# Second norm and first query moved into the output projection, queries of both block groups in one chain, and the gathered blocks' scores searched from SBUF

## The chip, the cores and the metric

The kernel runs on one core of a Trainium2 chip, as one program. The metric is the device time of one execution in microseconds (us). The engines are named as in the profile: PE is the matrix engine (PEld its weight loads), DVE the vector engine, ACT the scalar engine, POOL the GpSimd engine, and SP the engine that issues most of the DMAs. Each engine takes its instructions in the order of the program; semaphores join the engines.

## What is computed

One layer on 1024 tokens of width 1024, in float32. Two mixers (a gated linear recurrence and a chunked state-space scan) each give 512 columns; these are normed, multiplied by an output matrix and added to the input. Then follows a retrieval layer ("PEER"), which is what the change is about:

```python
h = h + y @ w_out                        # y: the two normed groups side by side
x = rms_norm(h, norm2_g)
q = (x @ wq).reshape(T, 8, 256)          # 8 heads, two halves of 128 each
s1 = einsum('thd,kd->thk', q[..., :128], k1)   # 128 scores for each half
s2 = einsum('thd,kd->thk', q[..., 128:], k2)
v1, i1 = top_k(s1, 16); v2, i2 = top_k(s2, 16)
sc, cidx = top_k(v1[..., :, None] + v2[..., None, :], 16)   # best 16 of the 256 pairs
e = i1[cidx // 16] * 128 + i2[cidx % 16]                    # an expert of 16384
g = softmax(sc)
out = sum over h, k of g * gelu(u_tab[e] . x) * v_tab[e]
result = rms_norm(h + out, normf_g)
```

## The kernel before, in words

**Tiling.** The tokens are 8 blocks of 128. Blocks 0 to 4 (`dblocks`, ND = 5) are dense blocks: all 16384 experts are computed for them by matmuls, with the chosen weights spread out as a matrix G. Blocks 5 to 7 (`gblocks`, NG = 3) are gathered blocks: for each token the 128 chosen rows of the two expert tables are fetched by POOL's indirect DMAs (2 x 128 transfers of 512 KB for a block, line 1146) and multiplied on DVE, with eight row buffers (`rows`). Every float32 product runs as three float32r matmuls, of a high and a low part; ACT makes the high part by a copy, DVE the low part by a subtraction (names ending in h and l).

**Order.** Each piece of work is a Python generator, and `Merge` (lines 62 to 118) interleaves several of them as the program is written: it keeps an estimated clock for each engine, and always takes the generator whose own clock plus a bias is lowest. A generator that yields a name waits until that flag is set. What stands in each engine's queue is fixed by this.

**Output projection** (`front`, lines 757 to 841). `wo_half` loads and splits the eight 128x512 pieces of one half of w_out, with ten buffers for the split pieces (tags woh and wol) and two for the raw ones (wor). `norm` gives the group's row factors rg (a matmul with ones into gs, then a root and small DVE steps). `w_out` goes through the blocks from 7 down to 0, two column halves each: 12 matmuls into wop, then DVE adds wop times rg into h. After the second half, ACT sums the squares of h[b] into ss (jk). The two PSUM buffers of wop are the tag pj.

**Second norm and queries** (`peer`, lines 856 to 972). All pools of `front` are closed first. `norm2` scales and transposes first blocks 5 to 7, then 0 to 4: rsqrt_cols on ss, xn on DVE (line 905), for the gathered blocks two stores (X_d, H_d), then eight PE transposes into x2t and the split into xGh and xGl, or xDh and xDl. `query` goes over 8 heads and two halves: weights (wqr by SP, split into wqh and wql one query ahead, two buffers), 24 matmuls into qp (twice for the dense blocks, 320 columns each), a copy to qt, and for each block two matmuls with the keys kT into sp, a copy to sc, and a store of sc to S_d in DRAM. It runs first for the gathered blocks (pool pqa), and after all pools of this stage have been closed a second time for the dense blocks (pool pqb).

**Choice** (`topk`, lines 983 to 1066). The 1 MB of a block's scores comes back from S_d (s). For each head and half, DVE finds the 16 largest of 128 (two rounds of MAX8 and FIND_INDEX8 with a MATCH_REPLACE8 between). Then it adds the candidate pairs (cd), searches them in the same way (scv, ci), and turns positions into indices with one-hot products (oh, if). For a gathered block the result is idx (flag g0 to g2), which the gathers wait for; for a dense block `build_g` transposes it, and makes 32 groups of one-hot matrices (ohA, ohB) for G. In the stage of the dense queries three threads run together: `dense_query`, `topks` (gathered blocks 5, 6, 7), and `gathers`. After it come `build`, the first layer of the dense experts for 97 of 128 tiles (`ahead`: ur, uh, ul, ap, stored as A_d), and at last the dense loop over 32 chunks (`dense`: vp), which takes in the remaining gathered rows.

Of the kernel before, what the change touches and what calls it, by code (L numbers as in the profile page):

```python
# [21 lines left out]
L = 8  # L22
# [127 lines left out]
def front(tc, a, cst, nd, mg):  # L150
# [608 lines left out]
    pools.close("fl", "fw", "fin", "fxa")  # L759
    pa_ = pools.open("fa")  # L760
    ah = pa_.tile([P, 4, T], F32R, name="ah")
    al = pa_.tile([P, 4, T], F32R, name="al")
    po = pools.open("fo")
# [4 lines left out]
    def wo_half(half):  # L768

        for k in range(4):  # L770
            for n in range(2):
# [39 lines left out]
    def w_out(half):  # L811
# [3 lines left out]
        for b in reversed(range(L)):  # L815
            bs = slice(b * P, b * P + P)
            for n in range(2):
                ns = slice(512 * n, 512 * n + 512)
                pp = pj("wop")
                for k in range(4):  # L820
                    wh, wl = wo[half][k, n]
                    PE.matmul(pp, dh[:, k, bs], wl, start=(k == 0), stop=False)
                    PE.matmul(pp, dl[:, k, bs], wh, start=False, stop=False)
                    PE.matmul(pp, dh[:, k, bs], wh, start=False, stop=(k == 3))
                yield
                V.scalar_tensor_tensor(h[b][:, ns], pp, rg[half][:, b:b + 1], h[b][:, ns], ALU.mult, ALU.add)
                yield
            if half:
                jk = po.tile([P, D], F32, name="jk", tag="sq2")
                S.activation(jk, h[b], AF.Square, accum_out=ss[:, b:b + 1])  # L830
                yield

    def group_a():
        yield from wo_half(0)
        yield from w_out(0)
        yield from wo_half(1)
# [19 lines left out]
def peer(tc, a, cst, pools, h, ss, mg):  # L856
# [9 lines left out]
    dr = pools.open("dram", space=DRAM)  # L866
    S_d = dr.tile([8, P, 8, 256], F32, name="S_d")
    X_d = dr.tile([NG, P, D], F32, name="X_d")
    H_d = dr.tile([NG, P, D], F32, name="H_d")
# [19 lines left out]
    pxg = pools.open("pxg")  # L889
    xGh = pxg.tile([P, 8, TG], F32R, name="xGh")  # L890
    xGl = pxg.tile([P, 8, TG], F32R, name="xGl")
    pn = pools.open("pn", "right", bufs=2)
    g2 = pn.tile([P, D], F32, name="g2", bufs=1)
    S.dma_start(g2, a["g2"].partition_broadcast(P))
    vv = pn.tile([P, 8], F32, name="vv", bufs=1)
    r2 = pn.tile([P, 8], F32, name="r2", bufs=1)
# [734 lines left out]
```

## Time and profile before

| | us |
|---|---|
| median of 3 runs (lowest, highest) | 2759.59 (2755.72, 2765.24) |
| the profiled execution, and its span | 2759.9, 2758.1 |
| busy in the span: PE, DVE | 2538.0 (92%), 2364.1 (86%) |
| busy in the span: ACT, POOL | 1329.9 (48%), 1164.7 (42%) |
| mean granted clock of PE | 0.964 of full speed |

How to read it: the profile is one execution, and times in it count from the start of its span. Nearly every instruction is issued through one helper and so carries the line L146; instructions are told apart by their tiles, written out<-in. "Idle before" is time in which the engine had nothing to do before an instruction, and the name behind it is what it waited for. The chain of waits is followed back from the last instruction of the program, at each step to what released it.

### The profile page before, as it was taken

What the parts mean: (1) busy time and instruction counts of PE and PEld (TensorE: products, weight loads), DVE (VectorE), ACT (ScalarE), POOL (GpSimd) and SP (SyncE); (2) the same over time, 40 slices, a digit from 0 to 9 for tenths busy, and PEclk for the clock granted to TensorE, in tenths of its full rate; (3) what the DMA queues carried; (4) which work ended last, traced back from release to release, by engine and by line L of the source; (5) the groups of instructions that cost most, each with busy time, mean ns of one, the idle gap of its engine ahead of it and who ended that gap; (6) DMA issues with size and microseconds to landing.
All of it is one profiled execution on the core that took longest, in us unless ns stands there. A gap on an engine that the chain in (4) does not pass through costs nothing.

```text
span 2758.1 us, 40787 instructions
## 1 busy us (share of the span) xinstructions
PE 2538.0 (92%) x14623; PEld 2289.4 (83%) x14623; DVE 2364.1 (86%) x4540; ACT 1329.9 (48%) x2407; POOL 1164.7 (42%) x777
## 2 busy tenths in 40 slices
PE   5979879887899999989989889999999999999997
PEld 5767769787898999988989878888788888888885
DVE  6888634699998999989989869999788889999996
ACT  5456424222294693955846734444443334434432
POOL 0000000044373575856836634455445555445550
PEclk9999889999999999999999999999999999999998
DMA  5111233375799898997998999999889999999993
GB/s 167 29 38 33 105 136 125 127 256 180 267 366 371 287 401 323 353 392 266 397 334 293 400 343 328 328 328 327 321 316 327 330 328 333 334 327 327 327 343 134
DMA packets 302139, 761.83 MB, mean 276 GB/s; under 512 B 28784, under 2 KB 126384, under 8 KB 296816
## 3 DMA queue, kind: packets, MB, share of 16 engines
q0 software_dynamic: 110592, 402.70, 40.8%
q1 hardware_dynamic: 184464, 345.19, 35.3%
q10 hardware_dynamic: 6880, 11.33, 1.2%
q8 instruction: 115, 1.88, 0.3%
q14 instruction: 88, 0.72, 0.1%
HBM read 668.81 MB, written 89.13 MB: 275 GB/s over the span
## 4 chain that ended last, share of the span: by engine, by line
PE 57%; DVE 25%; DMA 9%; issue 5%; ACT 3%; POOL 1%; SPq 0%; ACTq 0%; DVEq 0%; POOLq 0%
PE vp L146 24%; PE ap L146 15%; PE total L146 6%; DVE row L146 5%; PE wop L146 3%; PE qp L146 3%; DMA A_d<-aa 3%; PE gp L146 2%; DVE ix L146 2%; DVE oh L146 2%; DVE ul L146 2%; DMA ur<-in_uT_dram 2%; DVE v L146 2%; PE pj L146 1%; DVE hb L146 1%
## 5 line engine op out<-in xcount | busy, mean ns | idle before, releaser
L1146 POOL DMA_INDIRECT row<-in_peer_u_dram,idx x384 | 581.6, 1515 | 1014.4 <-DVE ix L146 521.6
L1146 POOL DMA_INDIRECT row<-in_peer_v_dram,idx x384 | 580.3, 1511 | 477.9 <-DVE hb L146 364.2
L146 PE MATMUL ap<-xDl,uh 128*128 128x320 f32 x2048 | 654.8, 320 | 16.3 <-ACT aa L146 16.1
L146 PE MATMUL ap<-xDh,ul 128*128 128x320 f32 x2048 | 650.5, 318 | 20.4 <-DVE ul L146 20.3
L146 PE MATMUL ap<-xDh,uh 128*128 128x320 f32 x2048 | 646.9, 316 | 0.0
L146 DVE SCALAR_TENSOR_TENSOR hb<-row,act,hb 128x1024 f32<-128x1024 f32 x384 | 492.2, 1282 | 6.6 <-DMA hb<-H_d 2.2
L146 DVE CUSTOM_DVE_ANT_0 row<-row,xg 128x1024 f32<-128x1024 f32 x384 | 458.5, 1216 | 7.7 <-DMA xg<-X_d 4.9
L146 PEld LDWEIGHTS ap<-xDh,ul 128*128 128x128 f32 x2048 | 392.2, 192 | 25.5 <-DVE ul L146 24.1
L146 PE MATMUL vp<-vl,hh 128*128 128x512 f32 x1024 | 400.3, 391 | 12.6 <-DVE h L146 10.4
L146 PEld LDWEIGHTS ap<-xDl,uh 128*128 128x128 f32 x2048 | 392.4, 192 | 19.7 <-ACT aa L146 17.7
L146 PE MATMUL vp<-vh,hl 128*128 128x512 f32 x1024 | 400.1, 391 | 0.0
L146 PE MATMUL vp<-vh,hh 128*128 128x512 f32 x1024 | 400.1, 391 | 0.0
L146 PEld LDWEIGHTS ap<-xDh,uh 128*128 128x128 f32 x2048 | 391.6, 191 | 0.0
L146 ACT ACTIVATE gq<-gt 128x640 f32<-128x640 f32 x128 | 175.1, 1368 | 337.7 <-DVE hr L146 335.8
L146 PE MATMUL gp<-ohB,ohA 128*128 128x128 f32 x1280 | 211.0, 284 | 43.0 <-ACT gs L146 24.8
L146 DVE TENSOR_TENSOR ul<-ur,uh 128x1024 fp32r<-128x1024 f32 x128 | 156.1, 1219 | 108.5 <-ACT uh L146 108.4
L146 PEld LDWEIGHTS vp<-vl,hh 128*128 128x128 f32 x1024 | 193.0, 188 | 54.1 <-DVE h L146 11.7
L146 PEld LDWEIGHTS gp<-ohB,ohA 128*128 128x128 f32 x1280 | 186.8, 194 | 52.8 <-ACT gs L146 27.0
L146 PEld LDWEIGHTS vp<-vh,hh 128*128 128x128 f32 x1024 | 193.0, 188 | 40.3
L146 PEld LDWEIGHTS vp<-vh,hl 128*128 128x128 f32 x1024 | 193.1, 189 | 39.4
L146 ACT ACTIVATE aa<-ap 128x320 f32<-128x320 f32 x194 | 85.0, 439 | 267.8 <-PE ap L146 250.1
L146 ACT ACTIVATE ohB<-ohB,kt 128x128 f32<-128x128 f32 x480 | 204.4, 503 | 0.0
(424 smaller groups left out, 4512.8 us busy)
## 6 DMA issues: line engine op xcount, KB each, us to landing
ur<-in_uT_dram SPq DMA_DIRECT2D x128, 512.0 KB, 6.6
vr<-in_peer_v_dram SPq DMA_DIRECT2D x128, 512.0 KB, 6.5
gt<-G_d SPq DMA_DIRECT2D x32, 1280.0 KB, 9.5
G_d<-gs SPq DMA_DIRECT2D x19, 2048.0 KB, 25.4
A_d<-aa SPq DMA_DIRECT2D x96, 320.0 KB, 7.4
hr<-A_d SPq DMA_DIRECT2D x96, 320.0 KB, 5.7
wqr<-in_wq_dram SPq DMA_DIRECT2D x32, 512.0 KB, 4.2
S_d<-sc SPq DMA_DIRECT2D x64, 128.0 KB, 3.7
```

Source lines behind the costliest of these rows:

```text
L146: return fn(*args, **kw)
L1146: G.indirect_dma_start(out=r, out_offset=None, in_=a["peer_v" if at >= P else "peer_u"], in_offset=bass.IndirectOffsetOnAxis(ap=idx[n][:, ...
```

## The change

1. **Projection.** The pool of the output weights is opened before that of ah and al, so that the latter can be closed after the first half. `wo_half` goes over columns first; the weights of the second half may be loaded once the first columns of the first half (flag cols0), or all of it (half0), have been used, and `w_out(0)` goes through all blocks for the first columns and then for the second.
2. **Norm and first query in `front`.** A new class `Norm2` holds the second norm. For blocks 7, 6 and 5 it runs beside the second half's lower blocks, as soon as flags h7 to h5 are set. `query0` loads the first of the 32 query weights into buffers of the output weights, and computes the first query of the gathered blocks (q0) behind the projection.
3. **One query chain.** `query` runs through the gathered and then the dense blocks, with weights loaded one query ahead across the seam. The norm of the dense blocks is a thread beside it.
4. **Search from SBUF.** The gathered blocks' scores are not stored to S_d; sc stays in one of six buffers, and the thread `found_g` searches head by head, into tiles vg and ixg kept for `topk`, which for these blocks starts with the candidates once flag "found" is set.
5. **Pools and biases.** rows, gp and pu lie on the other side of the memory; `topks` and `gathers` have the biases 1.0 and 2.0, and the dense query is no thread of this run.

The core of the diff (the changes of names and pools that only follow from it are left out):

```diff
     def wo_half(half):
-        for k in range(4):
-            for n in range(2):
+        for n in range(2):
+            for k in range(4):
+                if half:
+                    yield "half0" if (n, k) >= (1, 2) else "cols0"
...
-        for b in reversed(range(L)):
+        todo = [(b, n) for b in reversed(range(L)) for n in range(2)]
+        if half == 0:
+            todo.sort(key=lambda x: x[1])
+        for b, n in todo:
...
+            if half == 0 and (b, n) == (0, 0):
+                mg.flag("cols0")
+            if half and n:
                 jk = po.tile([P, D], F32, name="jk", tag="sq2")
                 S.activation(jk, h[b], AF.Square, accum_out=ss[:, b:b + 1])
+                mg.flag(f"h{b}")
                 yield
+        mg.flag(f"half{half}")
...
-    mg.run([(0.5, norm(0, yA, ah, al)), (1.0, group_a())])
-    pools.close("fo", "fa", "fgw", "fg", "fvt", "fkeep", "fps")
-    return pools, h, ss
+    mg.run([(0.5, norm(0, yA, ah, al)), (1.0, group_a()), (1.0, wo_half(1))], until="half0")
+    pools.close("fa")
+    nx = Norm2(tc, a, cst, pools, h, ss, mg)
+
+    def query0():
+        hi, lo = [], []
+        for i in range(2):
+            r = po.tile([P, 512], F32, name="wor", tag="wor", bufs=2)
+            nc.sync.dma_start(r.rearrange("p (k n) -> p k n", n=P), a["wq"][0][:, 4 * i:4 * i + 4])
+            yield "half0"
+            wh = po.tile([P, 512], F32R, name="woh", tag="woh", bufs=10)
+            wl = po.tile([P, 512], F32R, name="wol", tag="wol", bufs=10)
+            S.activation(wh, r, AF.Copy)
+            V.tensor_tensor(wl, r, wh.bitcast(F32), ALU.subtract)
...
+        yield "xg"
+        yield "half1"
+        p_ = pt("qp")[:, :TG]
+        for k in range(8):
+            PE.matmul(p_, hi[k], nx.xGl[:, k], start=(k == 0), stop=False)
+            PE.matmul(p_, lo[k], nx.xGh[:, k], start=False, stop=False)
+            PE.matmul(p_, hi[k], nx.xGh[:, k], start=False, stop=(k == 7))
+        yield
+        S.activation(nx.q0, p_, AF.Copy)
+        mg.flag("query0")
+
+    def norm2_g():
+        for b in range(ND, L):
+            yield f"h{b}"
+        yield from nx.run(list(range(ND, L)), nx.xGh, nx.xGl, pt)
+        mg.flag("xg")
...
+    mg.run([(0.5, norm2_g()), (1.5, query0_late())], until="query0")
+    mg.run([], until="half1")
...
+    def run(self, blocks, dh, dl, pt):
+        mg, nc, h = self.mg, self.tc.nc, self.h
+        sl = slice(blocks[0], blocks[-1] + 1)
+        rsqrt_cols(mg, self.vv[:, sl], self.r2[:, sl], self.ss[:, sl], 1.0 / D)
+        yield
+        for n, b in enumerate(blocks):
+            xn = self.pn.tile([P, D], F32, name="xn", tag="xn")
+            mg.V.scalar_tensor_tensor(xn, h[b], self.r2[:, b:b + 1], self.g2, ALU.mult, ALU.mult)
+            yield
+            if b >= ND:
+                nc.sync.dma_start(self.X_d[b - ND], xn)
+                nc.sync.dma_start(self.H_d[b - ND], h[b])
...
+        nxt = weights(1)
+        yield
+        for part, (blocks, dh, dl) in enumerate(((gblocks, nx.xGh, nx.xGl), (dblocks, xDh, xDl))):
...
+            if part:
+                mg.flag("qg")
+                yield "xd"
...
+                    sc = pq.tile([P, 256], F32, tag="sc", name="sc", bufs=6)
+                    S.activation(sc, p_[:, :256], AF.Copy)
+                    if part:
+                        nc.sync.dma_start(S_d[b, :, h_], sc)
+                    else:
+                        scs[h_, n] = sc
...
+    def found_g():
+        for h in range(8):
+            for n in range(NG):
+                yield lambda: (h, n) in scs
+                sc = scs.pop((h, n))
                 for f in range(2):
+                    top16(sc[:, f * P:(f + 1) * P], found[n][0][:, f, h], found[n][1][:, f, h])
                 yield
+        mg.flag("found")
+
+    mg.run([(0.0, norm2_d()), (0.5, query()), (1.0, found_g())], until="xd")
+    mg.run([], until="qg")
+    pools.close("pn", "pxg", "hg")
...
     def topk(b):
+        if b >= ND:
+            yield "found"
+            v, ix = found[b - ND]
...
-    mg.run([(0.0, dense_query()), (0.5, topks()), gr], until="q")
-    pools.close("pqb")
+    mg.run([(1.0, topks()), gr], until="q")
+    mg.run([], until="chosen")
+    pools.close("pkg", "pq")
```

What this does to the engines' queues is seen at two places. On PE, at the end of the output projection, the queue before has the 24 transposes of the gathered blocks' norm (x2t) behind the last projection matmul (wop, second half: gh, gl), and then the first query (qp) with its weights wqh and wql:

```order
L146 MATMUL wop<-wol,gh 128x512
L146 MATMUL wop<-woh,gl 128x512
L146 MATMUL wop<-woh,gh 128x512
L146 MATMUL x2t<-ident,xn 128x128 x24
L146 MATMUL qp<-xGl,wqh 128x384
L146 MATMUL qp<-xGh,wql 128x384
L146 MATMUL qp<-xGh,wqh 128x384
```

In the changed kernel the first 16 transposes stand in the middle of the second half:

```order
L146 MATMUL wop<-wol,gh 128x512
L146 MATMUL wop<-woh,gl 128x512
L146 MATMUL x2t<-ident,xn 128x128 x8
L146 MATMUL wop<-woh,gh 128x512
L146 MATMUL x2t<-ident,xn 128x128 x8
L146 MATMUL wop<-wol,gh 128x512
L146 MATMUL wop<-woh,gl 128x512
```

The last eight follow 13 matmuls behind these, and the projection's last matmul is followed directly by the first query, whose weights lie in buffers named woh and wol:

```order
L146 MATMUL wop<-woh,gl 128x512
L146 MATMUL wop<-woh,gh 128x512
L146 MATMUL qp<-xGl,woh 128x384
L146 MATMUL qp<-xGh,wol 128x384
L146 MATMUL qp<-xGh,woh 128x384
```

So the norm's transposes moved from behind the projection into it, and the first query moved up to its end. On DVE, the queue before searches the gathered scores only after all gathered queries, from the tile s that came back from DRAM, between weight splits (wql) of the dense queries, and goes on to the candidates (cd):

```order
L146 TENSOR_TENSOR wql<-wqr,wqh 128x1024
L146 MAX v<-s 128x8 x2
L146 MAX_INDEX ix<-v,s 128x8 x2
L146 MAX v<-s 128x8 x2
L146 MAX_INDEX ix<-v,s 128x8 x2
L146 MATCH_REPLACE s<-v,s 128x128 x2
L146 MAX v<-s 128x8 x2
L146 MAX_INDEX ix<-v,s 128x8 x2
```

In the changed kernel, in the middle of the gathered queries, one head of all three blocks is searched from sc (tiles vg_3311, vg_3313 and vg_3315) between two pairs of weight splits:

```order
L146 TENSOR_TENSOR wql<-wqr,wqh 128x1024 x2
L146 MAX vg_3311<-sc 128x8 x2
L146 MAX_INDEX ixg_3312<-vg_3311,sc 128x8 x2
L146 MATCH_REPLACE sc<-vg_3311,sc 128x128 x2
L146 MAX vg_3311<-sc 128x8 x2
L146 MAX_INDEX ixg_3312<-vg_3311,sc 128x8 x2
...
L146 MATCH_REPLACE sc<-vg_3315,sc 128x128 x2
L146 MAX vg_3315<-sc 128x8 x2
L146 MAX_INDEX ixg_3316<-vg_3315,sc 128x8 x2
L146 TENSOR_TENSOR wql<-wqr,wqh 128x1024 x2
```

So the search of the gathered scores moved ahead by the whole gathered query stage, with two weight splits before each head of it. Counted over DVE's whole queue, the third idx stands behind 22 gathered rows instead of 33, the first one-hot of the build behind 61 instead of 50, and the dense loop's first addition behind 398 instead of 393 (the first low part of v there behind 393 instead of 388).

More of the change, by code (lines that the diff above doesn't have):

```diff
@@ L886, in split_to, with norm2_d, query @@
         V.tensor_tensor(lo, src, hi.bitcast(F32), ALU.subtract)
[L889 to L896, printed above, removed]
[L898 to L927 removed]
+    pq = pools.open("pq", bufs=2)
+    def norm2_d():
+        yield from nx.run(dblocks, xDh, xDl, pt)
+        mg.flag("xd")
+    def query():
         kT = pq.tile([P, 2, P], F32, name="kT", bufs=1)
@@ new lines, in query, with top16 @@
+        mg.flag("q")
+    pkg = pools.open("pkg")
+    found = [(pkg.tile([P, 2, 8, 16], F32, name=f"vg{n}"), pkg.tile([P, 2, 8, 16], U32, name=f"ixg{n}"))
+             for n in range(NG)]
+    scs = {}
+    def top16(x, vals, at):
+        for r in range(2):
+            vs = vals[:, 8 * r:8 * r + 8]
+            V.max(vs, x)
+            V.max_index(at[:, 8 * r:8 * r + 8], vs, x)
+            if r == 0:
+                V.match_replace(x, vs, x, -3.0e38)
+    def found_g():
[3 more added lines that the diff above has]
+                sc = scs.pop((h, n))
@@ L962, in query @@
                 for f in range(2):
-                    PE.matmul(p_[:, f * P:(f + 1) * P], qs[f][:, n * P:(n + 1) * P], kT[:, f], start=True, stop=True)
+                    top16(sc[:, f * P:(f + 1) * P], found[n][0][:, f, h], found[n][1][:, f, h])
                 yield
-                sc = pq.tile([P, 256], F32, tag="sc", name="sc", bufs=4)
-                S.activation(sc, p_[:, :256], AF.Copy)
-                nc.sync.dma_start(S_d[b, :, h_], sc)
-                yield
-    pqa = pools.open("pqa", "right", bufs=2)
@@ L971, in peer @@
-    mg.run([(0.0, norm2()), (0.5, query(pqa, gblocks, xGh, xGl))])
-    pools.close("pqa", "pn", "hg", "pxg")
-    rows = pools.open("rows", bufs=ROWS)
-    gp = pools.open("gp", bufs=2)
-    pu = pools.open("pu", bufs=2)
+        mg.flag("found")
+    mg.run([(0.0, norm2_d()), (0.5, query()), (1.0, found_g())], until="xd")
+    mg.run([], until="qg")
+    pools.close("pn", "pxg", "hg")
+    rows = pools.open("rows", "right", bufs=ROWS)
+    gp = pools.open("gp", "right", bufs=2)
+    pu = pools.open("pu", "right", bufs=2)
@@ L1009, in topk @@
         for h in range(8):
[L1010 to L1016 removed]
+            top16(cd[:, h], sc[:, h], ci[:, h])
             yield
@@ L1562, in body @@
     cst = dict(ident=ident, iota=iota)
[L1563 to L1564 removed]
+    fpools, h, nx = front(tc, a, cst, ND, mg)
+    peer(tc, a, cst, fpools, h, nx, mg)
     pools.close("cst")
```

186 lines of the change are left out of this document (89 added, 97 removed).

## The prediction

> **What bounds the kernel now.** I read the busy time of the engines by stretches first, then the chain of waits through the stretches that the change touches, then the instructions there one by one. In the stretches the columns are start and end, length, busy time (and instructions) of PE, PEld, DVE, ACT and POOL, granted clock, DMA share and GB/s.
>
> ```profile
> 398.00:511.26 113.26, 93.86 (x544) 89.27 (x544) 41.50 (x55) 41.91 (x76) 0.00 (x0) 0.89 0.43 139
> 511.26:561.10 49.84, 44.23 (x285) 42.84 (x286) 49.55 (x251) 15.12 (x29) 0.00 (x0) 0.90 0.39 129
> 561.10:688.60 127.50, 104.80 (x693) 101.16 (x692) 126.62 (x510) 30.55 (x67) 56.06 (x37) 0.93 0.68 226
> 688.60:750.00 61.40, 52.59 (x327) 50.83 (x328) 61.40 (x250) 15.68 (x25) 19.22 (x18) 0.94 0.77 260
> ...
> 1200.00:1300.00 100.00, 95.52 (x644) 93.80 (x644) 97.25 (x287) 45.67 (x94) 57.32 (x29) 0.98 0.87 304
> 1300.00:1400.00 100.00, 86.67 (x600) 84.16 (x599) 84.98 (x152) 83.20 (x218) 71.35 (x49) 0.93 1.04 391
> ...
> 2000.00:2400.00 400.00, 396.42 (x1922) 341.00 (x1923) 357.40 (x471) 161.99 (x177) 207.12 (x142) 0.99 0.91 326
> ```
>
> Four regimes stand here. From 398 to 511 (norm and queries of the gathered blocks) DVE works 41.5 of 113.3 us, and PE has most of the work. From 511 to 750 DVE is never idle (176.2 of 177.3 us, then 61.4 of 61.4): it searches scores, and PE waits for it. From there to about 1640 DVE and PE are each near 90 to 97%, and in some stretches the DMA engines are full (1.04). After 1640 PE sets the time (396.4 of 400). So an idle DVE lies directly before a full one.
>
> The chain (start, length, what) shows what the idle stretch consists of:
>
> ```profile
> 349.03 4.03 DMA ur<-in_uT_dram
> 356.11 41.45 PE wop L146 x174
> 399.61 5.41 DMA g<-in_g_dram
> ...
> 406.36 5.20 DMA X_d<-xn
> ...
> 416.11 11.32 PE qp L146 x48
> ...
> 485.16 7.28 PE qp L146 x42
> 495.07 7.30 PE qp L146 x42
> 505.16 1.86 DMA S_d<-sc
> 507.21 6.53 DMA wqr<-in_wq_dram
> ...
> 562.32 4.24 DMA row<-in_peer_u_dram,idx
> ...
> 1640.94 12.28 PE vp L146 x54
> ```
>
> Output projection until 397.6, then a DMA and a norm with PE idle until the queries at 416.1; a gathered head takes 9.91 us (485.16 to 495.07); then a store and a weight load at the seam before the dense queries; the first gather only at 562.3, and the dense loop (vp) from 1640.9. Who waited there:
>
> ```profile
> PE qp L146 <- DVE wql L146: 22.5, 7, 9.6
> PE qp L146 <- ACT wqh L146: 10.2, 1, 10.2
> ...
> DVE v L146 <- DMA s<-S_d: 16.1, 1, 16.1
> ```
>
> **The change, part by part.** The sum is made against the profiled execution: span 2758.1 us, its own time 2759.9, which is 0.3 above the median of the runs (2759.59). I count how much earlier fixed places in the program are reached.
>
> The prices come from these rows: instructions in order of time (start, length, and idle before), then groups (shortest, median and longest ns), and one DMA issue with its us to landing.
>
> ```profile
> 397.16 0.39 PE L146 MATMUL wop<-woh,gh 128*128 128x512 f32 x1
> 421.08 0.52 PE L146 MATMUL qp<-xGl,wqh 128*128 128x384 f32 x1
> 421.40 0.52 PE L146 MATMUL qp<-xGh,wql 128*128 128x384 f32 x1
> 426.93 0.33 PE L146 MATMUL qp<-xGh,wql 128*128 128x384 f32 x1
> 427.10 0.34 PE L146 MATMUL qp<-xGh,wqh 128*128 128x384 f32 x1
> 427.27 1.03 PE L146 MATMUL x2t<-ident,xn 128*128 128x128 f32 x8
> 428.07 0.42 PE L146 MATMUL qp<-xGl,wqh 128*128 128x384 f32 x1
> ```
>
> ```profile
> 511.26 0.49 DVE L146 MAX8 v<-s 128x8 f32<-128x128 f32 x2 [16.09 <-DMA s<-S_d]
> ...
> 513.61 0.47 DVE L146 MAX8 v<-s 128x8 f32<-128x128 f32 x2
> ...
> 755.36 0.70 DVE L146 TENSOR_TENSOR ohA<-iota,kt 128x512 f32<-128x512 f32 x1
> ```
>
> ```profile
> L146 DVE SCALAR_TENSOR_TENSOR xn<-h,r,g x8: 1274/1283/1286, 405.0 to 440.4; 128x1024 f32<-128x1024 f32 x8
> L146 ACT ACTIVATE wqh<-wqr x32: 1047/1052/1071, 404.8 to 660.1; 128x1024 fp32r<-128x1024 f32 x32
> L146 DVE TENSOR_TENSOR wql<-wqr,wqh x32: 1193/1222/1251, 406.2 to 669.5; 128x1024 fp32r<-128x1024 f32 x32
> L146 DVE CAST idx<-if x3: 205/209/261, 561.1 to 688.6; 128x128 int32<-128x128 f32 x3
> L146 DVE CUSTOM_DVE_ANT_0 row<-row,xg x384: 1192/1217/1296, 566.6 to 2354.9; 128x1024 f32<-128x1024 f32 x192
> ```
>
> ```profile
> wqr<-in_wq_dram SPq DMA_DIRECT2D x32, 512.0 KB, 4.2
> ```
>
> *Weights of the second half.* The columns-first order frees four weight buffers early, and the ur loads leave this place, so the wait that ended at 356.1 can shrink. But the two splits of the first query's weights now stand ahead of the last step of the half's own rg on DVE, and behind that step wait both PSUM buffers of wop. Bounds: the seven microseconds from 349.0 to 356.1 gone, or 3 more. I take −2, nearer to nothing, because the same rg chain still ends it.
>
> *Norm inside the second half.* Its 24 transposes cost PE 3 × 0.80 (427.27 to 428.07) = 2.4 us among the wop matmuls. Added are waits: for xn of block 5 behind a square, a root and five small DVE steps, with 2 units of wop ahead on PE; and for the third xn, whose buffer is free only when the X_d store (5.20) landed. DVE stands still meanwhile, with the h update behind it that frees a wop buffer. I take +5 in all (bounds +2.4 and +11). The projection so ends at 397.6 − 2 + 5 = 400.6.
>
> *First query in front, next weights.* Its 24 matmuls follow at once. The next weights wait for the projection's end as the first did before: 0.5 to issue, 4.2 to land, 1.05 and 1.22 to split: 407.6. PE is idle about 3 us of it. The spacing of matmuls was 0.32 us after the 9 us gap (421.08 to 421.40) and 0.17 later (426.93 to 427.10), so the second query takes 7.7 us slow or 4.2 fast. I take 7.7: it ends at 415.3, where before both had ended at 427.3, 12 us earlier. The Trainium skill (TensorE: Matmul & The Clock Gate, What's actually happening) says that about 3.4 us of idleness halves the clock and as much work restores it. By that page the shorter gap may leave the clock up, and the place would be reached 3.5 us sooner; the trace shows only the long gap.
>
> *The seam.* Store, pool change and weight load between 502 and 514.9 go, as queries run on. PE then starts the dense queries at 514.9 − 12 − 11.5 = 491. It worked 44.2 + 104.8 = 149 us from 511.3 to 688.6; so the place of 688.6 comes at 640 at the earliest on PE, 49 sooner (53 with the fast clock).
>
> *Searches moved.* One head of one block takes 2.35 us (511.26 to 513.61); 24 of them, 56.4 us, move under the gathered queries. A head there costs DVE 3 × 2.35 + 2 × 1.22 = 9.5 us against PE's 9.91, so the cover just holds, and the norm of the dense blocks comes on top. DVE's work from 398 to 688.6 is 41.50 + 49.55 + 126.62 = 217.7. Out of it go 3 × 1.28 of xn, about 3.7 of the six xGl (taken as half a wql each) and 1.2 of the first split, all now ahead of the projection's end: 209. With 11 us idle (4 until the first weights land, 7 waiting for scores; bounds 4 and 30) DVE is at the place of 688.6 by 400.6 + 209 + 11 = 621, 68 sooner. If the cover failed, DVE would keep part of its old idle time. The stores and loads of S_d that go (24 and 3 on SP) lay in a stretch with DMA share 0.4.
>
> *After the third idx.* In the order, the first one-hot of the build (755.36) has 61 rows of the gather ahead of it instead of 50, so DVE is there 68 − 11 × 1.217 = 55 sooner. PE had 8.8 us idle in 688.6 to 750 and can be there 49 to 58 sooner. At the head of the dense loop 393 rows are done instead of 388: DVE could be 62 sooner, PE not more than 58. I take 55. The dense loop then has 5 rows less; PE sets it, so that is worth 0.
>
> Sum: 2759.9 − 55 = **2705**.
>
> **The rivals.** *Transfers set it.* The row gathers cannot begin before the first idx; searches end near 501 (400.6 + 41.5 − 8.7 + 56.4 + 11), and what followed them for block 5 took from 530 (511.3 + 8 × 2.35) to 561, so the first gather comes at 532, only 30 sooner. If bytes bound everything from there to 1640, the gain is 30: 2730. For it: 1.04 in 1300 to 1400. Against: 0.87 in the stretch before, 0.68 in 561 to 688. The Trainium skill (DMA: Bandwidth & Descriptors, Issuing engines are not separate DMA queues) says that all queues end on the same 16 engines, so gathers that start beside the query weights get no bandwidth of their own; by it this rival is what a full stretch would do.
>
> *Searches stop the queries: slower.* DVE takes its instructions in order. If a search stood ahead of the weight split that PE needs next, each gathered head would be in series: 9.91 + 7.05 + 1.22 = 18.2 instead of 9.91, 8 × 8.3 = 66 us more, 2705 + 66 = 2771. It decides from 9.91 + 55/8 = 16.8 us a head. Against it: two splits stand ahead of each head's searches in the order, and PE has two queries (8.3 us) to work on meanwhile.
>
> *Given back.* If the stretch from 755 to 1640 is held by the work that alternates there (PE, DVE and DMA each in turn the fullest), a start 55 sooner could end in more waits there: about 2757.
>
> *More.* With no extra waits in the projection and DVE setting all until 1640: 75 − 6 = 69 sooner, 2691.
>
> **How the numbers follow.** Forecast 0.70; transfers 0.15; more 0.06; given back 0.05; series 0.04. The likeliest gives 2705; the range takes in "more" (2691) and the transfers with their 6 us of five more rows (2736), and leaves 0.09 out, with some for the sum's own errors. A measurement of this kernel tells about 0.3% (8 us) from no change. Faster: 0.70 + 0.15 + 0.06 = 0.91; same 0.05; slower 0.04.
>
> **What would show it.** Right: DVE near 90% busy from 405 to 500; no PE gap at the seam; wop's end at 399 to 404; third idx near 621 and first one-hot near 700; vp from about 1586; the dense loop as long as before. Wrong: a gathered head over 12 us, wop ending past 408, or the 55 us present at the first one-hot but gone at the first vp.

## The result, and the profile after

The changed kernel takes **2685.56 us** (median of 4 runs, 2682.52 to 2690.74) against 2760.64 us for the kernel before on the same chip: a ratio of 0.9728, 95% interval 0.9706 to 0.9749, 75 us faster. The forecast was 2705, so the direction was right and the gain was 20 us larger than the sum gave; it also lies below the low end of 2691. The profiled execution has a span of 2683.4 us. Times here and below are medians of undisturbed executions: one of p19 and one of g48, at granted clocks of 0.557 and 0.840 where the others had 0.96 to 0.98, are left out.

First the places that the forecast named. The stretches after the change, with the columns of the prediction's first view (start and end, length, busy time of PE, PEld, DVE, ACT, POOL, clock, DMA share, GB/s), cut at the projection's end, the seam, the first idx, the third idx, the first one-hot and the first vp:

```profile
398.10:488.50 90.40, 85.92 (x513) 81.68 (x512) 83.18 (x377) 38.19 (x68) 0.00 (x0) 0.98 0.41 130
488.50:525.20 36.70, 35.74 (x252) 34.89 (x251) 36.13 (x168) 14.01 (x28) 0.00 (x0) 1.00 0.39 126
525.20:600.60 75.40, 71.11 (x470) 69.16 (x470) 75.05 (x226) 22.07 (x47) 39.73 (x30) 0.95 0.83 279
600.60:708.60 108.00, 96.99 (x630) 94.87 (x629) 97.72 (x315) 27.66 (x48) 56.02 (x40) 0.95 0.81 291
708.60:1567.40 858.80, 803.67 (x5591) 792.75 (x5590) 803.08 (x1855) 584.77 (x1418) 532.45 (x334) 0.97 0.98 355
1567.40:2683.40 1116.00, 1087.33 (x5283) 934.31 (x5281) 981.25 (x1083) 439.88 (x488) 541.70 (x367) 0.99 0.88 314
```

The idle stretch of DVE is filled: 83.2 of 90.4 us busy where it was 41.5 of 113.3. The same two last stretches of the kernel before, for comparison:

```profile
755.36:1640.80 885.44, 813.04 (x5593) 798.43 (x5593) 811.07 (x1873) 584.67 (x1418) 537.81 (x341) 0.96 0.96 349
1640.80:2758.10 1117.30, 1088.71 (x5281) 934.38 (x5280) 987.42 (x1088) 439.70 (x488) 545.06 (x372) 0.99 0.88 316
```

The dense loop is as long as before (1116.0 and 1117.3). The stretch from the first one-hot to the first vp is not: 858.8 instead of 885.4. The sum had the same 55 us at both of its ends, so it took the length as unchanged; 26.5 us of it are gone, and the first one-hot came 8 us later than forecast. Together that is most of the 20 us by which the sum fell short.

The matmuls at the projection's end (start, length, idle before):

```profile
397.72 0.39 PE L146 MATMUL wop<-woh,gh 128*128 128x512 f32 x1
397.95 0.34 PE L146 MATMUL qp<-xGl,woh 128*128 128x384 f32 x1
...
401.94 0.34 PE L146 MATMUL qp<-xGh,woh 128*128 128x384 f32 x1
403.54 0.44 PE L146 MATMUL qp<-xGl,wqh 128*128 128x384 f32 x1 [1.26 <-ACT q L146]
...
404.70 0.33 PE L146 MATMUL qp<-xGh,wqh 128*128 128x384 f32 x1
404.87 0.33 PE L146 MATMUL qp<-xGl,wqh 128*128 128x384 f32 x1
...
487.97 0.34 PE L146 MATMUL qp<-xGh,wqh 128*128 128x384 f32 x1
...
488.50 0.39 PE L146 MATMUL qp<-xDl,wqh 128*128 128x320 f32 x1
```

The projection ends at 398, the second query begins after a gap of 1.3 us, and the dense queries follow the gathered ones without a gap, at 488.5 where they had begun at 514.9.

The chain of waits after the change, through the same places:

```profile
461.23 7.28 PE qp L146 x42
471.11 7.28 PE qp L146 x42
481.02 7.30 PE qp L146 x42
526.44 4.50 DMA row<-in_peer_u_dram,idx
...
616.73 13.05 PE qp L146 x89
630.67 5.43 DMA S_d<-sc
636.16 10.68 DMA s<-S_d
708.69 4.18 ACT ohB L146 x12
...
1567.71 12.27 PE vp L146 x54
```

A gathered head still takes 9.9 us with a search inside. New in the chain are the last dense query, the store of its scores and their load for the first dense block's search (630.67 to 646.84): DVE, now ahead, meets PE's last scores. The search begins when they land:

```profile
646.87 0.49 DVE L146 MAX8 v<-s 128x8 f32<-128x128 f32 x2 [1.56 <-DMA s<-S_d]
```

### The profile page after: what moved, and what is told of

Its sections match the earlier page's. It is cut to its first block, busy times and chain, and to the rows that moved or that the text cites. A ratio compares the mean times of both kernels' runs of the same rounds, so it can differ in the third digit from the quotient of the medians.

```text
span 2683.4 us, 40720 instructions
## 1 busy us (share of the span) xinstructions
PE 2517.4 (94%) x14623; PEld 2276.8 (85%) x14623; DVE 2364.5 (88%) x4541; ACT 1330.2 (50%) x2408; POOL 1172.7 (44%) x777
## 4 chain that ended last, share of the span: by engine, by line
PE 60%; DVE 21%; DMA 9%; ACT 6%; issue 4%; ACTq 0%; SPq 0%; POOL 0%; DVEq 0%; POOLq 0%
PE vp L146 25%; PE ap L146 17%; PE total L146 6%; DMA A_d<-aa 4%; PE qp L146 4%; ACT ohB L146 3%; PE gp L146 3%; PE wop L146 3%; DVE row L146 2%; DVE oh L146 2%; DVE ul L146 2%; PE pj L146 2%; DVE hb L146 1%; DVE ix L146 1%; DMA nf<-in_gf_dram 1%
## 5 line engine op out<-in xcount | busy, mean ns | idle before, releaser
L1233 POOL DMA_INDIRECT row<-in_peer_u_dram,idx x384 | 562.6, 1465 | 961.0 <-DVE scv L146 495.6
L1233 POOL DMA_INDIRECT row<-in_peer_v_dram,idx x384 | 607.3, 1581 | 448.0 <-DVE hb L146 328.8
L146 PEld LDWEIGHTS ap<-xDl,uh 128*128 128x128 f32 x2048 | 392.5, 192 | 34.7 <-ACT aa L146 26.5
L146 PE MATMUL gp<-ohB,ohA 128*128 128x128 f32 x1280 | 198.1, 281 | 18.8 <-ACT gs L146 12.0
L146 PEld LDWEIGHTS gp<-ohB,ohA 128*128 128x128 f32 x1280 | 179.7, 193 | 24.4 <-ACT gs L146 13.3
```

Of the source, the lines that this page charges most:

```text
L146: return fn(*args, **kw)
L1233: G.indirect_dma_start(out=r, out_offset=None, in_=a["peer_v" if at >= P else "peer_u"], in_offset=bass.IndirectOffsetOnAxis(ap=idx[n][:, ...
```

## The experiments

The question: the prediction held that at the head of the dense loop DVE could be 62 us sooner but PE not more than 58, and took 55. Measured there (first vp) are 1640.8 − 1567.5 = 73. The step of the prediction (PE's place caps the stretch before vp) has two rivals: DVE's work sets it, or the transfers do. This table sums up all runs; each is told below. The texts set off ahead of each result are what was expected before the run. "Rows" are gathered rows ahead of the first one-hot, and ahead of the dense loop's first addition; the stretch runs from the first one-hot to the first vp, with DVE's and PE's busy time in it. The last column is against 2685.6.

| kernel | rows | first one-hot | first vp | stretch | DVE | PE | time | +us |
|---|---|---|---|---|---|---|---|---|
| before | 50, 393 | 755.4 | 1640.8 | 885.4 | 811 | 813 | 2760.6 | +75 |
| changed | 61, 398 | 708.6 | 1567.5 | 858.9 | 803 | 804 | 2685.6 | 0 |
| a0 (the same again) | 61, 398 | 706.0 | 1573.7 | 867.7 | 803 | 802 | 2685.8 | 0 |
| e1 (DVE work) | 55, 398 | 700.2 | 1597.9 | 897.7 | 834 | 820 | 2716.7 | +31 |
| e2 (PE work) | 62, 398 | 706.9 | 1568.7 | 861.8 | 802 | 825 | 2688.4 | +3 |
| e3 (loads, with a wait) | 61, 398 | 705.0 | 1679.7 | 974.7 | 805 | 831 | 2799.0 | +113 |
| e4 (copies) | 61, 398 | 722.8 | 1597.5 | 874.7 | 804 | 801 | 2714.0 | +28 |
| e5 (stores) | 61, 398 | 706.5 | 1591.1 | 884.6 | 804 | 810 | 2704.2 | +19 |
| p24 (fewer rows early) | 61, 344 | 706.2 | 1549.3 | 843.1 | 744 | 798 | 2699.5 | +14 |
| p19 (more rows early) | 61, 447 | 716.7 | 1667.5 | 950.8 | 863 | 831 | 2767.3 | +82 |
| u1 (search undone) | 54, 400 | 745.5 | 1636.7 | 891.2 | 814 | 817 | 2748.3 | +63 |
| u2 (norm, query undone) | 61, 398 | 713.4 | 1589.7 | 876.3 | 803 | 803 | 2699.6 | +14 |
| u3 (seam) | 61, 398 | 707.0 | 1572.1 | 865.1 | 803 | 801 | 2693.1 | +7 |
| u0 (u1, u2, u3) | 54, 400 | 752.6 | 1642.9 | 890.3 | 814 | 813 | 2760.6 | +75 |
| d15 (DVE later) | 61, 398 | 722.9 | 1592.5 | 869.6 | 802 | 804 | 2703.5 | +18 |
| d30 (DVE later) | 62, 398 | 732.5 | 1608.2 | 875.7 | 803 | 804 | 2711.2 | +26 |
| g24 (PE later) | 78, 398 | 730.1 | 1585.7 | 855.6 | 785 | 805 | 2700.6 | +15 |
| g48 (PE later) | 95, 398 | 758.6 | 1609.0 | 850.4 | 769 | 802 | 2728.4 | +43 |
| s4 (G in pieces) | 61, 398 | 709.0 | 1581.2 | 872.2 | 804 | 811 | 2699.1 | +14 |
| b24 (one-hots to ACT) | 61, 390 | 714.6 | 1657.7 | 943.1 | 757 | 837 | 2776.2 | +91 |

The runs were made on several chips, and the kernel before had medians of 2759.6 to 2767.7 beside them. The changed kernel took 2685.6 where the kernel before had 2760.6, and 2685.8 where it had 2767.3 (a0), which speaks for comparing times as they stand. By the ratios to the kernel before, against the changed kernel's 0.9728, the rows from chips with 2766 to 2768 come out smaller: u1 57, u0 69, u2 7, e5 9, d15 8, d30 14, s4 6 (e1 32 and e2 5 stay nearly the same). Such rows are therefore known to some 10 us only; a0, e5, u0 and p19 stood beside each other on one chip, and so did e1, e2, e3 and u3.

### Which engine sets the stretch before vp

**e1**, in each step of `ahead`:

```diff
+            pad = ph1.tile([P, 192], F32, name="pad", tag="pad", bufs=1)
+            some = xDh[:, 0, 0:192].bitcast(F32)
+            nc.vector.tensor_tensor(pad, some, some, ALU.add)
```

> The changed kernel with one more DVE instruction (a 128x192 tensor_tensor whose result nobody reads, about 0.26 us by 1.22 us for 1024 columns) at each of the 97 steps of the first dense layer: about 25 us more work for DVE between the first one-hot and the first vp. If PE's place caps that stretch (the step of the prediction: PE not more than 58 sooner), PE has the slack of DVE's waits: 0 to +3 us over the changed kernel's 2685.6. If DVE's work sets the stretch: +25. If transfers set it (DMA share 0.98 there): 0 to +5. If PE, DVE and DMA take turns: about a third to a half, +8 to +13.

Measured: ratio 0.9845 (0.9805 to 0.9886), +31 us. The group of the added instructions in its profile (busy, mean ns, idle before):

```profile
L1379 DVE TENSOR_TENSOR pad<-xDh 128x192 f32<-128x192 f32 x97 | 34.2, 353 | 0.1
```

They took 34.2 us rather than 25, and nearly all of it reached the end. The stretch, 30 to 39 us longer than in a0 and in the changed kernel:

```profile
700.20:1597.90 897.70, 820.22 (x5639) 802.69 (x5638) 833.52 (x1955) 586.23 (x1421) 522.88 (x340) 0.96 0.95 343
```

This is what "DVE's work" foresaw, and the cap by PE did not.

**e2**, in `first`:

```diff
             p_ = pa("ap")[:, :HALF]
+            if made[0] < NA:
+                nc.tensor.matmul(p_, uh[:, 0], xDh[:, 0, sl], start=True, stop=True)
             for k in range(8):
```

> The changed kernel with one more 320-column matmul in each half of the 97 steps of the first dense layer (194 matmuls, overwritten by the next one that starts the sum, so outputs are as before), about 0.147 us each, 28 us more work for PE between the first one-hot and the first vp. If PE's place caps the stretch: +28 us over 2685.6. If DVE's work sets it: 0 to +3. If transfers set it: 0 to +3. If they take turns: +9 to +14.

Measured: ratio 0.9745 (0.9704 to 0.9786), +3 us. Its stretch, from the first one-hot to the first vp:

```profile
706.90:1568.70 861.80, 825.05 (x5778) 817.44 (x5777) 802.03 (x1852) 587.51 (x1418) 534.08 (x333) 0.98 0.98 353
```

PE's idle time in it is 861.8 − 825.1 = 37 us, where the changed kernel has 858.9 − 803.8 = 55. PE took most of the added work in its waits: its place is no cap here.

**p24 and p19** change one number, the pace that the planner gives the gathered rows (in p19 to 1.9):

```diff
-PACE = 2.0
+PACE = 2.4
```

> The changed kernel with the planner's pace for the gathered rows at 2.4 instead of 2.0: 344 rows instead of 398 stand ahead of the dense loop's first addition, so 54 rows of 1.22 to 1.28 us, 67 us of DVE's work (and 27 MB), go from the stretch before vp into the dense loop. There PE sets the time and DVE was idle some 43 of 400 us. If DVE (or the transfers) set the stretch before vp: the first vp 50 to 67 us sooner, and the end by as much less what the dense loop does not hide: 2620 to 2650. If PE's place caps the stretch: the first vp 0 to 10 sooner, 2676 to 2690.

> The changed kernel with the planner's pace at 1.9: 447 rows instead of 398 stand ahead of the dense loop's first addition. The pace of 2.4 took 54 rows away there and made the first addition 17.5 us earlier and the dense loop 25 us longer. If both ways are alike: the first addition 16 us later, the dense loop 23 us shorter, 7 us faster than 2685.6. If DVE's work sets the stretch one for one as with 97 more instructions there: 60 us later against 23 to 30, 30 us slower.

Measured: p24 0.9786 (0.9744 to 0.9829), +14 us; p19 1.000 (0.9976 to 1.0024), +86 us. The stretch of p24:

```profile
706.20:1549.30 843.10, 797.92 (x5593) 789.16 (x5591) 743.83 (x1755) 585.36 (x1417) 434.72 (x279) 0.98 0.91 327
```

DVE has 59 us less to do and stands idle for 99 us; the stretch is only 16 us shorter than the changed kernel's, 25 than a0's. The first vp came 18 to 24 us sooner, which lies between the two forecasts (50 to 67, and 0 to 10). PE is not full in it either: of its 45 us of idleness 33 end with a step of DVE, so the two take turns. The stretch can thus be done in 843 us, and PE may need less. With 49 rows more (p19), it is 83 to 92 us longer, more than the 60 us of work that DVE has more, and neither forecast came. A row is work for DVE and a transfer of 512 KB at once, so these two runs do not tell DVE from the transfers. Neither pace helps, since the dense loop got 25 us longer with p24 (from the first addition to the last, 1118.0 against 1093.0) and no shorter to speak of with p19 (1089.0).

**g24 and g48** make PE late at the seam, by 163 and by 327 matmuls:

```diff
                         p_ = pa("qp")[:, :w]
+                        for _ in range(163 if at == 16 and i == 0 else 0):
+                            nc.tensor.matmul(p_, wh[:, 0], dh[:, 0, sl], start=True, stop=True)
```

> The changed kernel with 163 more matmuls of 320 columns, 0.147 us apart, ahead of the first dense query (overwritten by the first matmul of the sum): PE loses the 24 us there that the change had given it. The planner's order moves more rows of the gather ahead of the first one-hot (78 instead of 61), with the same 398 ahead of the first addition. If PE's place caps what follows (PE not more than 58 sooner): +15 to +24 us over 2685.6. If DVE's work carries the gain and PE's waits of 55 us in the stretch before vp take the loss in: 0 to +5.

> As the kernel with 24 us more for PE ahead of the first dense query, with 327 matmuls, 48 us: PE is later there than before the change. If PE's place caps what follows: +40 to +48. If DVE carries it and PE takes in what its 55 us of waits allow: 0 to +20.

Measured: g24 0.9771 (0.9752 to 0.9790), +15 us; g48 0.9879 (0.9836 to 0.9922), +43 us. Both times lie in the ranges given for a cap by PE's place (g24 at the lower end), and not in DVE's. PE's delay does reach the first one-hot, 21.5 and 50 us later, and g48 shows by which way (its first search of a dense block):

```profile
696.78 0.49 DVE L146 MAX8 v<-s 128x8 f32<-128x128 f32 x2 [0.90 <-DMA s<-S_d]
```

The first dense block's search waits for the scores of the last dense query, and so begins 50 us later than in the changed kernel. But DVE did not stand still: 95 rows are done by the first one-hot, not 61. The stretch behind it is therefore shorter, 850.4, with DVE idle for 82 us of it:

```profile
758.60:1609.00 850.40, 801.96 (x5596) 793.10 (x5596) 768.82 (x1787) 586.90 (x1418) 459.62 (x300) 0.97 0.94 338
```

So g48 has its first one-hot 3 us later than the kernel before, and yet its first vp 32 us sooner. Its time and DVE's idleness speak for PE's place as what sets the first vp here, with 48 us more in front of it. Such a cap then exists, but it does not lie at the prediction's 58. PE needs at most 843 to 850 us from the first one-hot to the first vp (p24 and g48), against 885.4 in the kernel before: there PE had at least 35 to 42 us of slack in that stretch.

### Transfers

**e3**, in each step of `ahead`:

```diff
+            pad = ph1.tile([P, 192], F32, name="pad", tag="pad", bufs=1)
+            nc.sync.dma_start(pad, a["uT"][j].rearrange("p a b -> p (a b)")[:, 0:192])
```

> The changed kernel with one more load of 96 KB (nobody reads it) at each of the 97 steps of the first dense layer: 9.5 MB, about 27 us at the 355 GB/s of that stretch. If PE's place caps it: 0 to +3 us over 2685.6. If DVE's work sets it: 0 to +3. If transfers set it: +27. If they take turns: +9 to +14.

Measured: 1.0129 (1.0084 to 1.0173), +113 us, four times what any theory gave. What SP's queue waited for (us in total, times, longest) tells why:

```profile
SPq L1318 <- DVE hl L146: 509.3, 93, 14.4
SPq L1378 <- DMA pad<-in_uT_dram: 289.0, 89, 9.6
```

With one buffer each load had to wait in SP's queue for the one before to land, and what stands behind it in that queue waited too: in the stretch before vp, ACT waited 65.1 us for the loads of ur, in the changed kernel 22.3. e3 measures a blocked queue, not bytes.

**e4**, at the same place:

```diff
+            nc.sync.dma_start(pad_d[j], a["uT"][j].rearrange("p a b -> p (a b)")[:, 0:192])
```

> The changed kernel with one more copy of 96 KB from DRAM to DRAM (nobody reads it, and its place is written once, so it waits for nothing) at each of the 97 steps of the first dense layer: the bytes of e3 without e3's wait of the issuing queue for the buffer of the load before. 9.5 MB, about 27 us at the 355 GB/s of that stretch. If transfers set it: +27 us over 2685.6, or more where reading and writing both count. If they take turns with DVE: +9 to +14. If DVE's work sets it: 0 to +4.

Measured: 0.9812 (0.9792 to 0.9832), +28 us, but not for the reason tested. As the copies wait for nothing, they stood at the start of SP's queue, among the first loads of the kernel; the first idx came at 539.4 instead of 525.2. So e4 is a kernel that is 14 us late before its searches are done; the rest lies in the stretch before vp, 7 to 16 us longer than in a0 and in the changed kernel, and that is not told apart from the difference between those two (9 us).

**e5**, behind the store of aa:

```diff
                 nc.sync.dma_start(A_d[j], t)
+                nc.sync.dma_start(pad_d[j], t[:, 0:192])
```

> The changed kernel with a second store of 96 KB of each aa, beside the store of A_d and ready with it, so that no new wait arises: 9 MB more in the stretch before vp, 26 us at 355 GB/s. If transfers set the stretch: +26 us. If DVE's work sets it: 0 to +4. If both in turn: +8 to +16.

Measured: 0.976 (0.974 to 0.978), +19 us. Its stretch:

```profile
706.50:1591.10 884.60, 809.60 (x5596) 798.50 (x5596) 803.62 (x1855) 583.88 (x1418) 520.41 (x334) 0.95 0.99 355
```

With DVE's work unchanged (803.6) the stretch is 17 to 26 us longer for 9 MB more, and the time is 18 us above that of a0 on the same chip, of the 26 us that the bytes would take. The DMA share is 0.99. So transfers count too, though not all of it need be bytes: the added stores did bring waits, since ACT waited 7.9 us for buffers of aa until they had landed. The Trainium skill (DMA: Bandwidth & Descriptors, Issuing engines are not separate DMA queues) says that transfers of all issuing engines end on the same 16 DMA engines; this run is in line with it, as 9 MB more of stores issued by SP made a stretch 17 to 26 us longer in which POOL gathers.

**s4** cuts the 2 MB stores of G:

```diff
-                if t0 + GT < TD:
+                if t4 < P - 4:
+                    late[:] = [lambda js=slice(i, i + 8): store(js) for i in range(0, P // JC, 8)]
+                elif t0 + GT < TD:
                     store(slice(0, P // JC))
```

> The changed kernel with the first three of each dense block's four stores of G (2 MB each, 25 us to landing) cut into four stores of 512 KB, one behind each of the next four groups of one-hots; bytes and work are the same. If waits behind these stores are what the stretch before vp still loses (24 us of ul, 12 of gp behind gs, 17 of ap behind aa): 10 to 30 us faster than 2685.6. If DVE's work alone sets it, or bytes do: within 4 us.

Measured: 0.975 (0.9724 to 0.9775), +14 us: no gain. The three waits named above were 30.6 us (ul), 9.3 (gp behind gs) and 19.9 (ap behind aa) in its profile: cutting the stores did not take them away.

### The parts of the change

**u1** stores all scores to S_d, has no thread `found_g`, and searches every block in `topk`:

```diff
-                    if part:
-                        nc.sync.dma_start(S_d[b, :, h_], sc)
-                    else:
-                        scs[h_, n] = sc
+                    nc.sync.dma_start(S_d[b, :, h_], sc)
...
-        if b >= ND:
-            yield "found"
-            v, ix = found[b - ND]
```

> The changed kernel with the gathered blocks' scores stored and searched after all gathered queries again, as before the change (norm, first query and seam as changed). If the searches are the main part of the gain: DVE begins its search about 9 us after the gathered queries' end at 488, so at 497 where before it began at 511, 14 us sooner than before: 2746. If PE's 23 us (12 at the second query, 11 at the seam) carry instead: 2737. If the searches are worth nothing: 2686 to 2690.

Measured: 0.9936 (0.9919 to 0.9952), +63 us (57 by the ratios). This is what the theory of the searches foresaw (2746; measured 2748), and the searches are the main part of the gain. The run undoes their place and their way over DRAM together, and does not tell these two apart.

**u2** puts the norm of blocks 5 to 7 and the first query back into `peer`:

```diff
-    mg.run([(0.5, norm2_g()), (1.5, query0_late())], until="query0")
...
+        yield from nx.run(gblocks, nx.xGh, nx.xGl, pt)
+        mg.flag("xg")
         yield from nx.run(dblocks, xDh, xDl, pt)
...
-        nxt = weights(1)
+        nxt = weights(0)
```

> The changed kernel with the gathered blocks' norm and the first query behind the projection again, in the stage of the queries (chain, seam and searches as changed). The queries start some 12 us later on PE and DVE has some 9 us of the norm and of a split again behind the projection's end. If DVE's work carries the gain: +12 to +20 us over 2685.6. If transfers or waits between 750 and 1640 give it back: 0 to +6.

Measured: 0.9753 (0.9729 to 0.9778), +14 us (7 by the ratios). It is undone only in part: the norm's first steps still ran during the projection, and the first query began at 403.1 instead of 398.0.

**u3** loads the first dense query's weights when the dense part begins:

```diff
                 mg.flag("qg")
                 yield "xd"
+                nxt = weights(16)
...
-                        if i == 0 and at < 31:
+                        if i == 0 and at < 31 and at != 15:
```

> The changed kernel with the seam between the gathered and the dense queries undone: the first weights of the dense queries are loaded only when the gathered queries have ended, so PE stands still there for about a load and a split, some 6 to 11 us, while DVE still has searches to do. If PE's place sets what follows (PE not more than 58 sooner in the prediction): +6 to +11 us over 2685.6. If DVE's work carries the gain: 0 to +3. If transfers set the rest: 0 to +3.

Measured: 0.9765 (0.9723 to 0.9806), +7 us, not told apart from nothing. And it did not do what it was for: the load was issued ahead of its place, and the dense queries began at 486.3, without a gap. Nothing follows from it for the seam.

**u0** has all three edits.

> The changed kernel with all three parts undone: searches after the gathered queries from DRAM, norm and first query behind the projection, weights at the seam loaded late. Undone singly they cost 57, 7 and 10 us by the ratios (0.9936, 0.9753, 0.9765 against 0.9728). If the parts add up and nothing else of the change matters: +75 us, ratio 1.00. If part of the gain comes from the rest (weights' order in the projection, pools, biases): ratio 0.99 or less. If DVE sets all and PE's parts count only beside the moved searches: 0.995.

Measured: 0.9978 (0.9963 to 0.9993), +75 us. The first matmul of its dense queries:

```profile
489.01 0.39 PE L146 MATMUL qp<-xDl,wqh 128*128 128x320 f32 x1
```

With the three parts undone all but some 6 us of the gain are gone, so the weights' order, the pools and the biases add little. PE begins the dense queries at 489.0, 26 us sooner than the kernel before, and 6 us by the ratio are left of this at the end. As long as DVE has the searches in front of it, PE's head start is worth little.

### One execution against another, and delays of DVE

> The changed kernel once more, unaltered, beside the others on the same chip: ratio 0.973 to the kernel before, and again a stretch of about 865 us from the first one-hot to the first addition if its short length belongs to the kernel; 875 to 885, as in six of the altered kernels, if it belonged to that one execution.

Measured: 0.9689 (0.9666 to 0.9711), 2685.75 us. The stretch took 867.7 us, where the first profile had 858.9, with the same work (DVE 802.7 and 803.2). Its line:

```profile
706.00:1573.70 867.70, 802.35 (x5593) 792.44 (x5592) 802.66 (x1855) 584.12 (x1418) 542.79 (x334) 0.96 0.97 351
```

To the first addition, where the expectation counted, it is 874.3 us after 865.5. So two executions of one kernel differ by 9 us there (and by 4.8 us in their spans, 2683.4 and 2688.2), and the very short stretch belonged to the first execution rather than to the kernel.

**d15 and d30** put 42 and 85 of e1's instructions ahead of the first one-hot.

> The changed kernel with 42 more DVE instructions of 0.353 us (nobody reads their result) ahead of the first one-hot: DVE is some 15 us later there and nothing else is changed. If the stretch from the first one-hot to the first vp has one length whatever its start, DVE's delay passes through: +15 us over 2685.6. If PE's place caps it: 0 to +5. If the stretch's waits behind transfers depend on how loads and stores happen to meet: anything between 0 and +35, with the stretch itself up to 20 us longer or shorter than the 865.5 from the first one-hot to the first addition.

> As the kernel with 15 us of delay, with 85 such instructions, 30 us. One length whatever the start: +30. PE's place caps it: +10 to +20. Chance meetings of transfers: +15 to +50, and the two delays not in proportion.

Measured: d15 0.9756 (0.9733 to 0.9779), +18 us; d30 0.9778 (0.9755 to 0.9801), +26 us. DVE's place at the first one-hot was 14 and 24 us later. By the medians all of this reaches the end, by the ratios against 0.9728 about half (8 and 14 us). For d15 either is more than the 0 to 5 of a cap by PE; beyond that the theories are not told apart.

**b24** gave the fourth of the four one-hots to ACT, with the pace at 2.4:

```diff
-                if e:
+                if True:
                     S.activation(B[:, e], iota, AF.Abs, bias=kt[:, 3, t:t + 1])
                 else:
                     V.tensor_scalar(B[:, e], iota, kt[:, 1, t:t + 1], kt[:, 2, t:t + 1], ALU.is_equal, ALU.mult)
...
-            for e in range(1, 4):
+            for e in range(4):
```

> The changed kernel with the fourth of each four second one-hots (160 on DVE, 0.34 us each, 0.25 apart) made by ACT as the other three are, and the planner's pace at 2.4 so that 390 rows instead of 398 stand ahead of the first addition: 40 to 54 us of one-hots and 10 us of rows less for DVE, 140 us more for ACT, which was busy 585 of 859 us. If DVE's work sets the stretch: the first vp 45 to 60 us sooner, 2626 to 2641. If PE (804 of 859 busy) or the transfers (0.98) stand close behind: 10 to 20 us sooner, 2665 to 2676. If ACT becomes the bound: 2690 to 2720.

Measured: 1.0029 (1.0011 to 1.0047), +91 us, worse than each theory gave. DVE has 46 us less work in the stretch and is idle for 186; PE waits for the one-hots of ACT and for splits that come later in the changed order. It rests on more than one thing, since the planner's order changed too, and it is left at that. Of s4, p24, p19 and b24, none beats the changed kernel.

## Why the prediction was right or wrong

**Searches moved: right.** The sum had 56.4 us for them; undoing them costs 57 to 63, and a gathered head stayed at 9.9 us with them inside.

**Norm in the projection: right, 2.5 us too dear.** Forecast end 400.6, measured 398.1. Its two terms (−2 and +5) are not measured singly.

**Second query: the slow clock did not come.** It was forecast to end at 415.3, and its last matmul starts at 408.3. The weights were a little quicker: the first matmul needs only the high part, and started at 403.5 instead of 407.6. And PE stood still for 1.3 us, where about 3 were forecast and the gap before the change was 9; matmuls were 0.17 us apart from 404.70 on, where they had been 0.32 apart behind the long gap. The Trainium skill (TensorE: Matmul & The Clock Gate, What's actually happening) puts the loss of clock at about 3.4 us of idleness; the traces agree, with 9 us that cost and 1.3 us that did not. The prediction weighed this and did not take it. Its price for the slow case was also too high: in the trace before, the slow spacing ended after 18 of the 24 matmuls of a query. So PE was 7 us ahead of the forecast here. How much of them reaches the end no run shows; a share like that of g24 (15 of 24) would make it some 4 us, which is an estimate.

**DVE at the third idx: right, 7 us short.** Forecast 68 us sooner than the place of 688.6. The third idx came 88.0 us sooner with 11 rows fewer ahead of it (22 instead of 33); with the time of these rows taken off, that is 88.0 − 11 × 1.217 = 74.6. Of the 6.6 us, 2.5 are the projection's end, 3 the idle time (8.1 of the 202.5 us from 398.1 to 600.6, where 11 was assumed), and the work was a microsecond less. That the third idx would stand "near 621" overlooked these 11 rows, which were known ahead of it from the order of the queue: with them its working gives 621 − 13.4 = 607.6.

**First one-hot: 8 us short.** Forecast 55 sooner, measured 755.4 − 708.6 = 46.8, which is 2 us below the 49 to 58 of PE's bound. By DVE's work alone it would have been 74.6 − 13.4 = 61. But DVE was idle for 10.3 us between the third idx and here, waiting for rows (7.5) and then for the scores of the last dense query (1.6), and it had some 4 us more work. That PE's place decides *here* is shown by g24 and g48.

**Head of the dense loop: the step that failed.** "DVE could be 62 sooner, PE not more than 58. I take 55." The first vp came 73.3 us sooner, and 67.1 in a0. The bound on PE was carried on from the first one-hot as if PE's way from there had a fixed length. It had not: PE was idle for 885.4 − 813.0 = 72 us of it, 52 of them until a copy on ACT was done and 20 until a step of DVE was, and p24 and g48 show that 843 to 850 us are enough for PE. So PE could have been 47 and another 35 to 42, some 82 to 89 us sooner. It was not the cap: the matmuls of e2, 28 us by estimate and 21 us more in PE's busy time, cost 3 to 5 us, 34 us more of work for DVE cost 31 (e1), and 9 MB more of stores cost up to 19 (e5). What set the first vp in the place of PE's 58 was DVE's work, with the transfers beside it; how the two share it is not divided by these runs. The 11 rows done early were no loss either, since they were work that the stretch then did not have (DVE busy 803 instead of 811).

In the prediction's terms, DVE's own figure, 62, with the 7 us of the third idx gives 69, and the measured 67 and 73 lie on either side of it. That it fits so well is partly luck, for two errors cancel. The sum has nothing for the time that DVE lost before the first one-hot, and nothing for a change of DVE's waits behind it. The 73.3 us are 46.8 at the first one-hot, 7.9 of work that the stretch no longer has, and 18.6 by which DVE's idleness in it fell (74.4 to 55.7 us); in a0 they are 49.4, 8.4 and 9.3. DVE's largest waits there (us in total, times, longest), with what ACT waited for ahead of one of them, before:

```profile
DVE ul L146 <- ACT uh L146: 36.4, 8, 11.2
ACT uh L146 <- DMA ur<-in_uT_dram: 35.3, 7, 11.7
DVE vl L146 <- ACT vh L146: 15.3, 1, 15.3
```

And after:

```profile
DVE ul L146 <- ACT uh L146: 24.0, 3, 13.4
ACT uh L146 <- DMA ur<-in_uT_dram: 22.3, 7, 10.5
DVE vl L146 <- ACT vh L146: 1.9, 1, 1.9
```

In a0 DVE's two were 20.0 and 12.1 us. So 9 to 19 us of the gain at the first vp are waits that no sum of the prediction had; why they grew shorter is not shown, and part of it belongs to the single execution.

**Dense loop: right.** 1116.0 against 1117.3.

**The rivals.** "More" named the right mechanism, DVE setting the time until the first vp with 69 sooner, and got 0.06; it too gave only 2691. But some 7 of its 69 us were waits left out in the projection, which ended 2.5 us sooner than the sum had it, so that its 69 also fits partly by luck. Transfers did not set the gain, though they cost in the stretch (e5): the first gather came at 526.4, 36 us sooner, and the end 75 sooner. No query was stopped by a search, and nothing was given back.

What stays open, too, is why the same instructions take 858.9 us in one execution of the stretch and 867.7 in the next, and 865 to 876 in the altered kernels with the same work (u2, u3, d15, d30, e4). Which load or store meets which was not followed up.

## What to carry to other kernels

A place that one engine cannot reach sooner is a cap only for what stands directly behind it; before it is carried on, its waits in the next stretch have to be taken off, since an engine that waits there can catch up. Where work can float between stretches (here the gathered rows), the place alone says little: count the work done by then, on the engine that has none to spare. And an engine that idles directly before a stretch whose length hangs on its work is worth filling, here at about one us for each us of work moved (56.4 moved, 57 to 63 gained).

## What the runs showed of the hardware that was not expected

A load that waited for its own buffer cost far more than its bytes: 97 loads of 96 KB, with 289 us of waiting in SP's queue, made the kernel 113 us longer (e3), while 9 MB of stores with next to no waits (7.9 us) cost 19 us (e5). And DVE's 128x192 addition took 353 ns each in e1, where 0.26 had been reckoned from the 1.22 us of an instruction with 1024 columns. By columns alone its share would be 0.23 us.
